# A fourth seven-product part and two overlapping GDN chains in a hybrid decoder layer on one Trainium2 core

## Chip, core and metric

The kernel runs on one core of a Trainium2 chip. The core has five engines with a queue of instructions each: PE (matrix products, with its weight loads shown as PEld), DVE (VectorE), ACT (ScalarE), POOL (GpSimd) and SP (SyncE, here only DMA issues). SP, ACT and POOL issue DMAs; 16 DMA engines carry them. The metric is the time of one execution on the device in microseconds (us), lower is better; 0.2% of it is 5.3 us.

## What is computed

One layer of a decoder trunk for 512 tokens and 2048 channels, in float32. Cut to what the change touches:

```python
h = _rmsnorm(x, norm_mix[l]) * (1.0 + sc_a) + sh_a
p = h @ w_in[l]                               # 2048 x 9296
c_q, c_kv, k_pe, q_g, k_g, v_g, z, b_logit, a_logit, gate_logits = _split_cols(p)
y_a = _mla_branch(c_q, c_kv, k_pe, ...) @ w_o_mla[l]
qkv = jnp.concatenate([q_g, k_g, v_g], axis=-1)          # 3 x 1024 columns, 8 heads of 128
y_b = _gdn_branch(qkv, z, b_logit, a_logit, ...) @ w_o_gdn[l]
...
def _gdn_branch(qkv, z, b_logit, a_logit, conv_w, ...):
    qkv = _causal_conv_silu(qkv, conv_w)      # width 4, along the tokens, per channel
    q, k = _l2norm(...), _l2norm(...)
    o = _gated_delta_chunked(q, k, v, beta, g)
    ...                                       # norm, times silu(z)

def _gated_delta_chunked(q, k, v, beta, g):
    ...
    Lmat = jnp.where(strict, jnp.einsum('bhncd,bhnsd->bhncs', kb, k) * decay, 0.0)
    sol = lax.linalg.triangular_solve(Lmat + I, rhs, lower=True, unit_diagonal=True)
    attn = jnp.where(lower, jnp.einsum('bhncd,bhnsd->bhncs', q, k) * decay, 0.0)
    def step(S, inp):                         # a scan over the chunks
        v_new = u_c - w_c @ S
        o = (q_c * exp(G_c)) @ S + a_c @ v_new
        S = S * exp(G_last) + k_dec.T @ v_new
```

After the two branches come the sigmoid gates, the output product, and a SwiGLU block that takes the second half of the time.

## The kernel before

**How it is written.** A Python program writes the whole instruction list. A matrix product is a list of *units* (`Unit`): a load of a weight tile, its split into a rounded part `hi` and a rest `lo` (ACT casts `hi`, DVE subtracts `lo`), and the matmuls, three for each pair of tiles (hi x hi, hi x lo, lo x hi). `Driver.run` writes the units in order, with loads and splits some units ahead (`drv.ahead`, `drv.deep`). Beside the units run *chains*, Python generators: after every 12 weighted matmuls (`GROUP`; a unit's `weight` is 1, `FAST` = 4/3, or 2) `pump` steps each chain once, and what the chain writes lands in the instruction order at that place. `yield n` in a chain is a pause of n pumps. `Score.order` then fixes the order on DVE and ACT with a model of times; PE, POOL and SP keep the written order.

**Interleaved loads.** `mixed` puts the units that read `w_mod` and some columns of `w_in` for the layer's modulation vectors (tiles `rawm`, `rawa`) between the others, at the pace of the table `PLAN`: pairs of (units before index n, such loads per unit). There are 160 of them.

**Buffers.** 68 tiles of 128 x 512 (`slots`), 5 weight tiles of 128 x 1024 (`raws`), 4 each for `hi` and `lo`, 8 PSUM banks. A tile's place is free again when its last reader is done, a store to DRAM included. The activations `hN` hold 32 of the 68 slots until gb3.

**Two ways to multiply.** A *plain set* (`w_in_fm`) makes 512 columns feature-major: 8 units of 24 matmuls, 192 in all, each 128 x 128 by 128 x 512. A *seven-product part* (`tokens_in`) makes 1024 columns token-major with seven block products in place of eight: 8 units of 4 products (24 matmuls) and 8 of 3 (18), 336 in all. A part's sums of weight blocks are made on DVE; one block sum goes out to `s_dram` from POOL and comes back. It uses sums and differences of the activations (`x56`, `x3`, parts of `hN`), which the part marked `last` gives up; `restore` then brings the overwritten halves of `hN` back.

**Order before** (`mixing`, line 2173 on): ga8, ga12; gb0 with the narrow set kb; three parts (latent queries and keys/values; Z; first halves of GDN queries and keys); then plain sets v03, q47, k47, v47, gb1, gb2, gb3; then the products of the attention (qpe, v0, v1, qk), ya, yb and the output product. In the names, 03 is heads 0 to 3 and 47 heads 4 to 7.

**GDN.** The token-major first halves of queries and keys stay in SBUF and are turned by 32 PE transposes (`inT`) at the start of v03. Convolved tiles (`conv_tile`, one per pump) of heads 0 to 3 stay in SBUF, those of heads 4 to 7 go to `cv_dram` and come back. `gdn(g)` is the chain of four heads: per chunk of 128 tokens it turns keys and queries (`pk`, `pq`), makes `kdec`, then turns values (`vp`), makes the decays `E`, the matrices `LT` and `AT`; then a solve of 31 steps on DVE (`fsX`, `fsT`), small products that build the inverse (`M1`, `X1`, `M2`, `X2`, `TT`), and a scan over the four chunks (`pks`, `r`, `pqs`, `py`, `yd`, `pS`, `po`, `o`). `kdec`, `vp`, `AT`, `kT` and `qT` stay in SBUF from start to end. The chain of heads 0 to 3 starts at v03, that of heads 4 to 7 in gb1, and `gated_out` follows each.

Of the kernel before, what the change touches and what calls it, by code (L numbers as in the profile page):

```python
# [16 lines left out]
P = 128  # L17
T = 512
NT = 4
# [265 lines left out]
class Score:  # L285
# [13 lines left out]
    def __init__(self, tc):  # L299
        self.tc = tc  # L300
        self.ops = []

    def engine(self, name):

        score, real = self, getattr(self.tc.nc, name)

        class Writer:
            def __getattr__(self, f):
                call = getattr(real, f)
                return lambda *args, **kwargs: score.ops.append(Op(name, f, call, args, kwargs))  # L310

        return Writer()
# [180 lines left out]
def block_kernel(ctx: ExitStack, tc: tile.TileContext, a: dict, out):  # L493
# [30 lines left out]
    def side(dst, src, **kw):  # L524
        nc.gpsimd.dma_start(dst, src, **kw)
# [354 lines left out]
    def conv_tile(idx, p):  # L880
        acc = S("cv")
        nc.scalar.activation(acc[:], p[:], AF.Copy, scale=cw[:, 72 + idx:73 + idx])
        for w in (2, 1, 0):
            sft = 3 - w
            nc.vector.scalar_tensor_tensor(acc[:, sft:], p[:, :T - sft], cw[:, 24 * w + idx:24 * w + idx + 1],
                                           acc[:, sft:], op0=ALU.mult, op1=ALU.add)
        nc.scalar.activation(acc[:], acc[:], AF.Silu)
        if idx % 8 < 4:
            conv_out[idx] = acc
        else:  # L890
            side(cv_dram[idx // 8, idx % 4], acc[:])
            conv_out[idx] = None

    cv_dram = dram.tile([3, 4, P, 512], F32, name="cv_dram")

    def conv_back(j):
        res = []
        for i in range(4):
# [22 lines left out]
    ba = C("ba", [P, NT, 16])  # L921
    kpe = C("kpe", [P, NT, 64])
    hspill = dram.tile([8, 2, P, 256], F32, name="hspill")

# [154 lines left out]
    fso = [dram.tile([4, NT, 4, 32, 32], F32, name=f"fso{g}") for g in range(2)]  # L1079

    def gdn(g):
        hd = slice(4 * g, 4 * g + 4)
        def conved(*parts):
            while not all(8 * j + 4 * g + i in conv_out for j in parts for i in range(4)):
                yield

        yield from conved(0, 1)
        while "eG" not in G:
            yield
        if g:  # L1090
            kT, qT = conv_back(1), conv_back(0)
            yield 5
        else:
            qT, kT = ([conv_out.pop(b + i) for i in range(4)] for b in (0, 8))
            yield 2

# [10 lines left out]

        kdec, vp, LT, AT = [], [], [], []
        for c in range(NT):
            pk, pq = tr4(kT, c, "pk"), tr4(qT, c, "pq")  # L1110
            kd = S("kdec")
            nc.vector.tensor_tensor(h4(kd[:]), h4(pk[:]), bc(G["eS"][:, c, hd], P), ALU.mult)
            kdec.append(kd)
            sumsq(pk[:], ssk[:, c, hd])
            sumsq(pq[:], ssq[:, c, hd])
            yield
# [14 lines left out]

        nxt = decays(0)
        yield from conved(2)
        vT = conv_back(2) if g else [conv_out.pop(16 + i) for i in range(4)]
        yield 3 if g else 1
        for c in range(NT):
            pv = tr4(vT, c, "pv")
            v = S("vp")
            nc.vector.tensor_tensor(h4(v[:]), h4(pv[:]), bc(nk_[:, c, hd], P), ALU.mult)
            vp.append(v)  # L1140
            eh, el = nxt
            if c < NT - 1:
                nxt = decays(c + 1)
            yield
            pe = PS("pE")
# [22 lines left out]
            nc.gpsimd.tensor_tensor(h4(at[:]), h4(at[:]), tri4, ALU.mult)  # L1168
            AT.append(at)
        del vT  # L1170
        fsL = []
# [10 lines left out]
        nc.gpsimd.memset(fsX_[64:128, 256:512:17], 1.0)  # L1182
        yield 2
        for j in range(31):
# [9 lines left out]
        del fsX_, fsX, fsT, fsL  # L1194
        T32 = S("T32")
# [53 lines left out]
        for hf in range(2):  # L1249
# [8 lines left out]
            M2.append(m2)  # L1258
        yield 6
        for hf in range(2):  # L1260
# [9 lines left out]
        del T64, T64T, T32, T32T, M1, M2, LT  # L1270
        yield
        Sst = S("Sst")
        for c in range(NT):
            if c:
                pks = PS("pks")
# [3 lines left out]
                for i in range(4):  # L1279
                    nc.vector.scalar_tensor_tensor(r[:, tok(i)], pks[:, tok(i)], G["eG"][:, c, 4 * g + i:4 * g + i + 1],  # L1280
                                                   vp[c][:, tok(i)], op0=ALU.mult, op1=ALU.subtract)
                pqs = PS("pqs")
# [6 lines left out]
            else:  # L1289
                r = vp[0]  # L1290
            py = PS("py")
# [7 lines left out]
            if c < NT - 1:  # L1299
                pS = PS("pS")  # L1300
                for i in range(4):
                    mm(pS[:, tok(i)], kdec[c][:, tok(i)], yd[:, tok(i)], start=True, stop=True)
                for i in range(4):
# [6 lines left out]
            for i in range(4):  # L1310
                mm(po[:, tok(i)], AT[c][:, tok(i)], yd[:, tok(i)], start=True, stop=True)
            o = S("o")
# [870 lines left out]
    def mixing():  # L2183
        yield act(load_scalars)
        for first, n in ((8, 4), (12, 4)):
# [7 lines left out]
            yield from us  # L2193
        us = w_in_fm("gb0", O_GB, gate_done(0), order=K_ORDER)
        for i, u in enumerate(us):
            def ahead(i=i):
                if i == 0:
                    for k in range(KT):
                        hT[k] = None
                while hN[K_ORDER[min(i + 2, 7)] + 1] is None:  # L2200
                    drv.step(chains["h"])
            with_pre([u], ahead)
# [12 lines left out]
        yield from tokens_in(0, O_CQ, c_out)  # L2215
        yield from tokens_in(1, O_Z, z_out)
        first = {}

        def first_out(t, f, src):
            dst = src  # L2220
            if src.tensor.name.startswith("m"):
                x = S("qk")
                dst = x[:]
                nc.scalar.copy(dst, src)
            first[t, f] = dst

        def turned_in():
            for f in range(2):
                for i0 in (0, 2):
                    both = [PS("inT") for _ in range(2)]  # L2230
                    for i, p in enumerate(both, i0):
                        for t in range(NT):
                            nc.tensor.transpose(p[:, tok(t)], first[t, f][:, tok(i)], ident)
                    conv_start(8 * f + i0, both)
                    yield
                for t in range(NT):
                    del first[t, f]
        yield from tokens_in(2, O_Q, first_out, O_K, lambda: drv.add(turned_in()), last=True)

        def start_conv():  # L2240
            drv.ahead = LOADS
            chains["conv"] = drv.add(conv_gen())
        us = with_pre(w_in_fm("v03", O_V, conv_done(16)), start_conv)
        with_pre(us[1:], gdn_sums)

        def start_a():
            ch["A"] = drv.add(gdn(0))
            drv.add(gated_out(0))
        with_pre(us, start_a)
        for u in us[4:]:  # L2250
            u.weight = FAST
        yield from us
# [4 lines left out]
        def start_b():  # L2257
            ch["B"] = drv.add(gdn(1))
            drv.add(gated_out(1))
        us = w_in_fm("gb1", O_GB + 512, gate_done(1), weight=FAST)  # L2260
        with_pre(us[2:], start_b)
        yield from us
        yield from w_in_fm("gb2", O_GB + 1024, gate_done(2), weight=FAST)
        us = w_in_fm("gb3", O_GB + 1536, gate_done(3), weight=FAST)
        for i, u in enumerate(us):
            def free(i=i):
                hN[2 * i] = hN[2 * i + 1] = None
            with_post(u, free)
            if i in (2, 4):
                with_pre([u], lambda i=i: chains.__setitem__(("q", "kv")[i // 2 - 1], drv.add(lora("q", n_qa) if i == 2 else lora("kv", n_kva))))  # L2270
        yield from us
# [1002 lines left out]
```

## Time and profile before

| | us |
|---|---|
| median of 3 runs | 2657.86 |
| lowest, highest | 2654.96, 2660.13 |
| profiled execution | 2656.74 |
| its span, first to last instruction | 2655.0 |
| granted TensorE clock in it | 0.999 |

From the starts of their first and last matmuls the stages of interest stand so in the profiled execution:

| stage | us |
|---|---|
| gb0 with kb | 188 to 243 |
| three seven-product parts | 243 to 473 |
| v03, q47, k47, v47 | 473 to 673 |
| gb1, gb2, gb3 | 673 to 841 |
| qpe, v0, v1 | 844 to 883 |
| qk, and ya | 883 to 1091 |
| scan of the first GDN chain (`py` to `po`) | 685 to 724 |
| scan of the second | 894 to 938 |

Lines of the profile name an engine, an operation, and what is written from what (out<-in). All of them carry line 483, where every recorded operation is issued, so tiles are told apart by name. A group has its count, busy time, mean length in ns, and the idle time before it with what ended it. A plain set's matmuls are `q`, `k`, `v` and `gb`, those of a part are `m`.

### The profile page before, as it was taken

The numbers are of one execution on the slowest core, as the hardware profiler recorded it, in microseconds if no ns is written. First come the engines' busy times: TensorE is split into PE (matmuls) and PEld (weight loads), VectorE is DVE, ScalarE is ACT, GpSimd is POOL, SyncE is SP. The second block draws the span as 40 slices with busy tenths as digits, with TensorE's granted clock in tenths as the row PEclk, the third lists the DMA queues.
The fourth block names the chain that finished last, engine by engine and source line by source line (L and its number), as shares of the span: only waits on it lengthen the run. The fifth ranks groups of instructions, "written<-read, shape, count | busy, mean of one in ns | idle before, by whom it ended". The sixth has DMA issues, their size and how long they took to land.

```text
span 2655.0 us, 36603 instructions
## 1 busy us (share of the span) xinstructions
PE 2635.5 (99%) x12668; PEld 2192.8 (83%) x12668; DVE 2215.8 (83%) x3401; ACT 1292.6 (49%) x1986; POOL 220.6 (8%) x369
## 2 busy tenths in 40 slices
PE   9999999999999999999999999999999999999998
PEld 7888888888888898888888888888888888888887
DVE  8988888878688688888997888888887888877888
ACT  4355444634535675234573444444444445445445
POOL 0000101011021000000100000000000101010000
PEclk9999999999999999999999999999999999999999
DMA  9985778755577447936854667766666667686795
GB/s 353 349 281 182 244 263 279 244 159 187 199 244 231 126 166 264 332 108 214 305 179 145 230 238 240 254 231 232 227 226 201 215 226 273 199 267 209 230 300 203
DMA packets 319986, 614.37 MB, mean 231 GB/s; under 512 B 45748, under 2 KB 74740, under 8 KB 319800
## 3 DMA queue, kind: packets, MB, share of 16 engines
q1 hardware_dynamic: 275064, 507.24, 58.0%
q0 software_dynamic: 24944, 78.97, 8.3%
q10 hardware_dynamic: 19792, 25.83, 2.9%
q8 instruction: 99, 1.62, 0.3%
q14 instruction: 87, 0.71, 0.1%
HBM read 518.55 MB, written 92.30 MB: 230 GB/s over the span
## 4 chain that ended last, share of the span: by engine, by line
PE 81%; issue 6%; DMA 5%; DVE 5%; ACT 2%; POOL 0%; ACTq 0%; SPq 0%; DVEq 0%; POOLq 0%
PE m L483 51%; PE v L483 4%; PE gu L483 3%; PE yb L483 3%; PE ya L483 3%; DMA raw<-in_w_in_dram 3%; PE gb L483 3%; PE q L483 2%; PE dn L483 2%; PE k L483 2%; PE dnt L483 2%; PE qk L483 2%; DVE lo L483 1%; DVE rawm L483 1%; ACT hi L483 1%
## 5 line engine op out<-in xcount | busy, mean ns | idle before, releaser
L483 ACT CAST hi<-raws 128x512 fp32r<-128x512 f32 (+1 forms) x448 | 409.1, 915 | 630.9 <-PE m L483 314.8
L483 DVE TENSOR_TENSOR lo<-raws,hi 128x512 fp32r<-128x512 f32 (+1 forms) x448 | 464.4, 1055 | 149.4 <-ACT hi L483 144.5
L483 ACT CAST hi<-raw 128x1024 fp32r<-128x1024 f32 (+2 forms) x199 | 201.9, 1017 | 306.4 <-DMA raw<-in_w_in_dram 75.1
L483 DVE TENSOR_TENSOR lo<-raw,hi 128x1024 fp32r<-128x1024 f32 (+2 forms) x199 | 234.1, 1181 | 62.5 <-ACT hi L483 60.6
L483 PE MATMUL m<-hi,xh 128*128 128x512 f32 x672 | 261.7, 389 | 1.2 <-ACT euvw L483 1.1
L483 PE MATMUL m<-hi,xl 128*128 128x512 f32 x672 | 261.4, 389 | 0.0
L483 PE MATMUL m<-lo,xh 128*128 128x512 f32 x672 | 261.4, 389 | 0.0
L483 ACT CAST hi<-sums 128x1024 fp32r<-128x1024 f32 x152 | 159.7, 1052 | 134.7 <-PE m L483 119.1
L483 DVE TENSOR_TENSOR lo<-sums,hi 128x1024 fp32r<-128x1024 f32 x152 | 185.6, 1221 | 38.0 <-ACT hi L483 38.0
L483 DVE CUSTOM_DVE_ANT_0 rawm<-rawm,cbc 128x1024 f32<-128x1024 f32 x160 | 195.3, 1238 | 15.3 <-DMA rawm<-in_w_mod_dram 15.0
L483 DVE TENSOR_TENSOR sums<-raws,raws 128x1024 f32<-128x1024 f32 x152 | 185.6, 1221 | 20.9 <-DMA raws<-in_w_down_dram 9.1
L483 PE MATMUL m<-hi,h2h 128*128 128x512 f32 x480 | 188.7, 393 | 0.0
L483 POOL DMA_DIRECT2D s_dram<-raws x152 | 82.3, 541 | 1263.5 <-DVE raws L483 1239.5
L483 PE MATMUL m<-hi,h2l 128*128 128x512 f32 x480 | 187.0, 389 | 0.0
L483 PE MATMUL m<-lo,h2h 128*128 128x512 f32 x480 | 186.8, 389 | 0.0
L483 PEld LDWEIGHTS m<-hi,xh 128*128 128x128 f32 x672 | 126.2, 188 | 28.2 <-ACT euvw L483 2.0
L483 PEld LDWEIGHTS m<-hi,xl 128*128 128x128 f32 x672 | 126.1, 188 | 26.3
L483 PEld LDWEIGHTS m<-lo,xh 128*128 128x128 f32 x672 | 126.2, 188 | 26.0
L483 DVE TENSOR_TENSOR raws<-raws,raws 128x512 f32<-128x512 f32 x152 | 103.2, 694 | 26.8 <-DMA raws<-in_w_down_dram 9.6
L483 DVE TENSOR_TENSOR raws<-sums,raws 128x512 f32<-128x512 f32 x152 | 104.6, 688 | 1.9
L483 PEld LDWEIGHTS m<-hi,h2l 128*128 128x128 f32 x480 | 90.1, 188 | 18.9
L483 PEld LDWEIGHTS m<-lo,h2h 128*128 128x128 f32 x480 | 90.2, 188 | 18.1
(555 smaller groups left out, 6396.3 us busy)
## 6 DMA issues: line engine op xcount, KB each, us to landing
raws<-in_w_gate_up_dram SPq DMA_DIRECT2D x400, 256.0 KB, 4.0
rawm<-in_w_mod_dram SPq DMA_DIRECT2D x160, 512.0 KB, 5.6
raw<-in_w_in_dram SPq DMA_DIRECT2D x95, 512.0 KB, 5.2
raws<-in_w_down_dram SPq DMA_DIRECT2D x160, 256.0 KB, 5.0
s_dram<-raws POOLq DMA_DIRECT2D x152, 256.0 KB, 3.7
raws<-s_dram SPq DMA_DIRECT2D x152, 256.0 KB, 3.9
raws<-in_w_in_dram SPq DMA_DIRECT2D x120, 256.0 KB, 4.3
raws<-in_w_o_dram SPq DMA_DIRECT2D x80, 256.0 KB, 4.1
```

Source lines behind the costliest of these rows:

```text
L483: self.tc.keep_in_program_order(op.call(*op.args, **op.kwargs))
```

## The change

The second halves of queries and keys (q47, k47) become a fourth part. The parts' order is now: latents; first halves; second halves; Z (which is `last`). The results of the two q/k parts go to `p_dram`, and one chain (`turn_first`), which starts at the tenth unit of Z, reads them back and turns them with 64 transposes. v03 takes gb0's place beside kb, and gb0 comes after v47 with weight `FAST`. All 24 convolved tiles are stored; first-half queries and keys are used from SBUF first, and all chains read values, and later queries and keys again, from DRAM. Both GDN chains are added at v47. Each stores `kdec`, `vp` and `AT` (11 tiles; the last chunk's `kdec` is no longer made) and drops `kT` and `qT` after the front, and reads them back for the scan. The set `mid` orders them: the second begins when the first is in the third of four chunks, the second's inverse when the first's scan is in its third chunk. `pause` waits for so many ns of matmul time by the planner's count. `PLAN` gets new paces, and the two latent chains start at gb3's units 0 and 3 in place of 2 and 4.

```diff
@@ conv_tile
-        if idx % 8 < 4:
-            conv_out[idx] = acc
-        else:
-            side(cv_dram[idx // 8, idx % 4], acc[:])
-            conv_out[idx] = None
+        side(cv_dram[idx // 8, idx % 8], acc[:])
+        conv_out[idx] = acc if idx in (0, 1, 2, 3, 8, 9, 10, 11) else None
@@ gdn
+        def keep(j, c, t):
+            side(gdn_dram[g, j, c], t[:])
+        def back(c):
+            res = []
+            for j in (0, 1, 2) if c < NT - 1 else (0, 1):
+                x = S(("vp", "AT", "kdec")[j])
+                nc.scalar.dma_start(x[:], gdn_dram[g, j, c])
+                res.append(x)
+            return res
-        while "eG" not in G:
+        while "eG" not in G or (g and "loops" not in mid):
             yield
+        while g and 0 not in mid:
+            yield
+        vT = conv_back(2, g)
...
+            if c == NT - 2:
+                mid.add("loops")
...
-        del vT
+        del vT, kT, qT, v, at, kd, eh, el, nxt, E, lt
+        mid.add(g)
...
-        yield 2
+        yield from pause(10000.0)
         for j in range(31):
...
-            if j % 4 == 3:
+            if j % 8 == 7:
                 yield
+        yield from pause(34000.0)
...
-        yield 24 if g else 22
+        yield from pause(11000.0)
+        while g and "second" not in mid:
+            yield
...
-        yield 6
+        yield 1
+        while not (g or 1 in mid):
+            yield
+        kT, qT, cur = conv_back(1, g), conv_back(0, g), back(0)
+        yield 5
...
         for c in range(NT):
+            if c == 2 and not g:
+                mid.add("second")
+            vp, AT, kdec = cur if c < NT - 1 else cur + [None]
+            if c < NT - 1:
+                cur = back(c + 1)
@@ plan
-    PLAN = ((17, 2.0), (33, 0.0), (81, 0.4), (89, 2.0), (113, 0.5), (137, 1.2), (143, 1.0), (156, 0.0), (175, 1.8), (1000, 1.2))
+    PLAN = ((17, 2.0), (33, 0.0), (89, 0.4), (97, 0.0), (113, 0.5), (137, 1.5), (143, 1.0), (156, 0.0), (175, 2.0), (1000, 1.5))
@@ mixing
-        us = w_in_fm("gb0", O_GB, gate_done(0), order=K_ORDER)
+        us = w_in_fm("v03", O_V, conv_done(16), order=K_ORDER)
...
-        yield from tokens_in(1, O_Z, z_out)
-        yield from tokens_in(2, O_Q, first_out, O_K, lambda: drv.add(turned_in()), last=True)
+        def turned_in(n, f, base):
+            rows = []
+            for t in range(NT):
+                x = S("tk")
+                nc.scalar.dma_start(x[:], p_dram[n, f, t])
+                rows.append(x)
+            yield 5
+            for i0 in (0, 2):
+                both = [PS("inT") for _ in range(2)]
+                for i, p in enumerate(both, i0):
+                    for t in range(NT):
+                        nc.tensor.transpose(p[:, tok(t)], rows[t][:, tok(i)], ident)
+                conv_start(base + i0, both)
+                yield 3
+        def turn_first():
+            yield from turned_in(0, 0, 0)
+            yield from turned_in(0, 1, 8)
+            gdn_sums()
+            yield
+            yield from turned_in(1, 0, 4)
+            yield from turned_in(1, 1, 12)
+        yield from tokens_in(1, O_Q, part_out(0), O_K)
+        yield from tokens_in(2, O_Q + 512, part_out(1), O_K + 512)
+        us = tokens_in(3, O_Z, z_out, last=True)
+        with_pre(us[9:], lambda: drv.add(turn_first()))
+        yield from us
...
-        yield from w_in_fm("q47", O_Q + 512, conv_done(4), weight=FAST)
-        yield from w_in_fm("k47", O_K + 512, conv_done(12), weight=FAST)
-        yield from w_in_fm("v47", O_V + 512, conv_done(20), weight=FAST)
+        def start_gdn():
+            drv.ahead = LOADS
+            for g in range(2):
+                ch["AB"[g]] = drv.add(gdn(g))
+                drv.add(gated_out(g))
+        yield from with_pre(w_in_fm("v47", O_V + 512, conv_done(20), weight=FAST), start_gdn)
+        yield from w_in_fm("gb0", O_GB, gate_done(0), weight=FAST)
+        yield from w_in_fm("gb1", O_GB + 512, gate_done(1), weight=FAST)
```

More of the change, by code (lines that the diff above doesn't have):

```diff
@@ L301, in __init__ @@
         self.ops = []
+        self.time = 0.0
     def engine(self, name):
@@ L309, in __getattr__, with record @@
                 call = getattr(real, f)
-                return lambda *args, **kwargs: score.ops.append(Op(name, f, call, args, kwargs))
+                def record(*args, **kwargs):
+                    op = Op(name, f, call, args, kwargs)
+                    score.ops.append(op)
+                    score.time += op.pace if op.pe else 0.0
+                return record
         return Writer()
@@ L887, in conv_tile, with conv_back @@
         nc.scalar.activation(acc[:], acc[:], AF.Silu)
-        if idx % 8 < 4:
-            conv_out[idx] = acc
-        else:
-            side(cv_dram[idx // 8, idx % 4], acc[:])
-            conv_out[idx] = None
-    cv_dram = dram.tile([3, 4, P, 512], F32, name="cv_dram")
-    def conv_back(j):
+        side(cv_dram[idx // 8, idx % 8], acc[:])
+        conv_out[idx] = acc if idx in (0, 1, 2, 3, 8, 9, 10, 11) else None
+    cv_dram = dram.tile([3, 8, P, 512], F32, name="cv_dram")
+    def conv_back(j, g):
         res = []
-        for i in range(4):
+        for i in range(4 * g, 4 * g + 4):
             x = S("cv")
@@ L1079, in block_kernel, with pause @@
     fso = [dram.tile([4, NT, 4, 32, 32], F32, name=f"fso{g}") for g in range(2)]
+    def pause(ns):
+        until_ = score.time + ns
+        while score.time < until_:
+            yield
+    gdn_dram = dram.tile([2, 3, NT, P, 512], F32, name="gdn_dram")
+    mid = set()
     def gdn(g):
         hd = slice(4 * g, 4 * g + 4)
+        def keep(j, c, t):
[7 more added lines that the diff above has]
+            return res
         def conved(*parts):
@@ L1132, in gdn @@
         nxt = decays(0)
-        yield from conved(2)
-        vT = conv_back(2) if g else [conv_out.pop(16 + i) for i in range(4)]
-        yield 3 if g else 1
+        yield 4
         for c in range(NT):
@@ L1194, in gdn @@
         del fsX_, fsX, fsT, fsL
+        yield from pause(7000.0)
         T32 = S("T32")
@@ L1301, in gdn @@
                 for i in range(4):
-                    mm(pS[:, tok(i)], kdec[c][:, tok(i)], yd[:, tok(i)], start=True, stop=True)
+                    mm(pS[:, tok(i)], kdec[:, tok(i)], yd[:, tok(i)], start=True, stop=True)
                 for i in range(4):
@@ L2215, in mixing @@
         yield from tokens_in(0, O_CQ, c_out)
-        yield from tokens_in(1, O_Z, z_out)
[L2217 to L2237, printed above, removed]
@@ L2253, in mixing, with part_out, output @@
-        yield from w_in_fm("q47", O_Q + 512, conv_done(4), weight=FAST)
-        yield from w_in_fm("k47", O_K + 512, conv_done(12), weight=FAST)
-        yield from w_in_fm("v47", O_V + 512, conv_done(20), weight=FAST)
[L2257 to L2262, printed above, removed]
+        def part_out(n):
+            def output(t, f, src):
+                dst = src
+                if src.tensor.name.startswith("m"):
+                    x = S("qk")
+                    dst = x[:]
+                    nc.scalar.copy(dst, src)
+                side(p_dram[n, f, t], dst)
+            return output
```

47 lines of the change are left out of this document (20 added, 27 removed).

## The prediction

> **What bounds the kernel now.** I read the page's busy table first, then the shares of the chain that ended last, then that chain in order of time.
>
> ```profile
> span 2655.0 us, 36603 instructions
> PE 2635.5 (99%) x12668; PEld 2192.8 (83%) x12668; DVE 2215.8 (83%) x3401; ACT 1292.6 (49%) x1986; POOL 220.6 (8%) x369
> PE 81%; issue 6%; DMA 5%; DVE 5%; ACT 2%; POOL 0%; ACTq 0%; SPq 0%; DVEq 0%; POOLq 0%
> ```
>
> PE is busy all along and carries 81% of the chain. That alone does not say that fewer matmuls are less time, since a modelled end can hide a wait. The chain in order of time does (start, length, what, how many):
>
> ```profile
> 476.28 0.87 PE inT L483 x8
> 479.90 0.87 PE inT L483 x8
> 484.18 0.87 PE inT L483 x8
> 487.80 0.87 PE inT L483 x8
> 580.54 43.52 PE k L483 x192
> 1178.89 76.22 PE m L483 x336
> 1493.47 68.02 PE m L483 x300
> ```
>
> 300 matmuls take 68.02 us, 192 take 43.52, 336 take 76.22: 226.7 ns each in every one, over 40 us and more on end. PE streams at a fixed pace there. The first four rows are all 32 transposes that turn the first halves of queries and keys: 8 in 0.87 us, 109 ns each. The view of what PE waited for, from 300 to 1010 us, says how much is not streaming:
>
> ```profile
> PE gb L483 <- DVE lo L483: 1.2, 2, 0.8
> PE py L483 <- DVE r L483: 1.1, 1, 1.1
> PE pT L483 <- ACT P L483: 1.0, 2, 0.7
> PE m L483 <- ACT up L483: 0.8, 1, 0.8
> PE sc L483 <- ACT P L483: 0.4, 1, 0.4
> PE m L483 <- DVE lo L483: 0.3, 1, 0.3
> ```
>
> In all 4.8 us out of 710 (columns: total, times, longest). So what is to be won is PE instructions, and waits can give back only a few us. What the other engines have left, by stretches (PE, PEld, DVE, ACT, POOL busy; clock; DMA share; GB/s):
>
> ```profile
> 0.00:100.00 100.00, 96.34 (x410) 77.56 (x411) 84.94 (x163) 45.20 (x60) 3.80 (x11) 1.00 0.96 350
> 243.00:319.00 76.00, 76.00 (x339) 62.98 (x338) 62.88 (x91) 38.20 (x48) 6.46 (x12) 1.00 0.66 225
> 319.00:396.00 77.00, 75.93 (x334) 62.06 (x333) 64.90 (x78) 34.56 (x43) 7.21 (x14) 1.00 0.78 267
> 396.00:473.00 77.00, 77.00 (x342) 63.75 (x341) 66.90 (x79) 34.62 (x43) 12.54 (x16) 1.00 0.83 283
> 440.00:473.00 33.00, 33.00 (x148) 27.31 (x147) 29.51 (x38) 15.72 (x21) 3.23 (x2) 1.00 0.91 307
> 473.00:842.00 369.00, 367.82 (x2069) 310.23 (x2068) 298.73 (x586) 177.17 (x400) 53.53 (x67) 1.00 0.65 207
> ```
>
> 243 to 473 are the three seven-product parts of now, 473 to 842 the seven plain sets from v03 to gb3 with the first GDN chain and the front of the second. The granted clock is 1.00 in each, so no count below needs a clock.
>
> **The change, part by part.**
>
> *Products.* The sets q47 and k47 go: 2 x 192 matmuls, 2 x 43.52 = 87.04 us. A fourth part comes: 8 units of 4 products and 8 of 3, each x 2 token tiles x 3 matmuls, 336 in all, 76.22 us. Its token-major results have to be turned, 32 transposes more, 4 x 0.87 = 3.48 us. Sum on PE: -87.04 + 76.22 + 3.48 = **-7.34 us**. That gb0 and v03 change places, Z comes last of the parts and the GDN matmuls move changes no PE count.
>
> *Waits of a part.* The `up` and the `lo` wait of `m` above, 1.1 us, are those of three parts: +0.4 for a fourth.
>
> *VectorE.* What a part costs it, from the page's groups, with the group that goes, from the groups of 476 to 930 us:
>
> ```profile
> L483 DVE TENSOR_TENSOR lo<-raws,hi 128x512 fp32r<-128x512 f32 (+1 forms) x448 | 464.4, 1055 | 149.4 <-ACT hi L483 144.5
> L483 DVE TENSOR_TENSOR lo<-sums,hi 128x1024 fp32r<-128x1024 f32 x152 | 185.6, 1221 | 38.0 <-ACT hi L483 38.0
> L483 DVE TENSOR_TENSOR sums<-raws,raws 128x1024 f32<-128x1024 f32 x152 | 185.6, 1221 | 20.9 <-DMA raws<-in_w_down_dram 9.1
> L483 DVE TENSOR_TENSOR raws<-raws,raws 128x512 f32<-128x512 f32 x152 | 103.2, 694 | 26.8 <-DMA raws<-in_w_down_dram 9.6
> L483 DVE TENSOR_TENSOR raws<-sums,raws 128x512 f32<-128x512 f32 x152 | 104.6, 688 | 1.9
> L483 DVE TENSOR_TENSOR lo<-raw,hi 128x1024 fp32r<-128x1024 f32 x67 | 81.5, 1222 | 24.0 <-ACT hi L483 23.5
> L483 DVE CUSTOM_DVE_ANT_0 rawm<-rawm,cbc 128x1024 f32<-128x1024 f32 x27 | 34.7, 1292 | 4.7 <-DMA rawm<-in_w_mod_dram 4.7
> ```
>
> A part has 8 each of the middle four and 24 of the first: 8 x (1.221 + 1.221 + 0.694 + 0.688) + 24 x 1.055 = 55.9 us, and 8 corrections of PSUM results, which I put at 0.69 like the nearest row (an estimate), 5.5: 61.4. Gone are 16 splits of q47 and k47, 16 x 1.222 = 19.6, and two `kdec` products, 1.4. So +40 us beside PE work. From 243 to 842 us VectorE is busy 62.88 + 64.90 + 66.90 + 298.73 = 493 of 599 us. The new pace table holds about 10 of the interleaved loads of `w_mod` back to after the queries' and keys' stage (34 + 0.4 x 56 + 0.5 x 16 + 1.5 x 24 + 6 = 106 by then, against 116): 10 x 1.29 = -13. Both chains now end about where gb3 ends, which brings the second chain's tail in, some 20 us on both VectorE and PE. Then (493 + 40 - 13 + 20) / (599 - 7 + 20) = 540 of 612, 88% where it was 82%. From 440 to 473 us it runs at 29.51 of 33, 89%, and PE is at 33.00 of 33: I cost it at nothing, and what hides it is the matmul stream. Without that cover it costs up to the whole 40.
>
> *DMA.* A part moves 48 loads and 8 stores of 0.262 MB, 14.7 MB, where two sets load 8.4: +6.3. Stores from POOL: 16 of the two parts' rows, 12 more convolved tiles, 22 GDN tiles; loads on ACT's queue: 16 rows, 20 more convolved tiles, 22 GDN tiles. That is 108 x 0.262 = 28.3 MB. Ten loads less of 0.524 are -5.2. From 243 to 842 us the rows give 76 x 0.225 + 77 x 0.267 + 77 x 0.283 + 369 x 0.207 = 136 MB; with +29 it is 165 in 612 us, 270 GB/s. Parts run without a wait at 283 and 307, the first 100 us reach 350. On average it is covered. The pinch is the end of the fourth part, below.
>
> *Issue and order.* The view of the tile `cv_dram`, the nearest to all these copies:
>
> ```profile
> L483 POOL DMA_DIRECT2D cv_dram<-cv x12: 539/542/583, 587.9 to 682.5; - x12
> L483 ACTq DMA_DIRECT2D cv<-cv_dram x12: 326/404/1750, 681.6 to 721.2; - x12
>   ACT yd L483: 3.7, 1
> DMA to landing us min/median/max: 2.3/3.3/7.4
> ```
>
> POOL gets 50 x 0.542 = 27 us more, ACT's queue 58 x 0.404 = 23; SP 32 more issues for the part. POOL is busy 53.5 of 369 us and ACT 177, so both have room. The added wait is that of an ACT load for the store of its tile to land. Behind it on ACT stand the casts `hi` of the next weights, and PE waits for these one or two units (5 to 10 us) later. Stores are issued tens of us before their load, except for the last four convolved tiles: between 0 and the 3.7 us that ACT `yd` once waited, on ACT alone; on PE I take 0.
> A store from POOL has a rule against it: the Trainium skill, "SBUF — State Buffer", Who interferes with whom, says that POOL cannot write a DMA's descriptors while a VectorE operation in a two-port mode holds the shared port, and gives 620 ns grown to 3100 beside a copy. By it 50 stores would land up to 2.5 us later each, an estimate from that page, and the time would be the slower rival's below instead of the sum's. The trace has no such gap in the issue (539 to 583 ns), only the spread of the landings, 2.3 to 7.4.
>
> *The chains.* The second starts when the first has two chunks of its front left, instead of after it. Its scan then no longer lies under the `qk` units, where `py` waited 1.1 us for `r` and `pT` 1.0 for `P`: -2.1. Against that, the solve of the second chain cost PE the 1.2 us of `gb` on `lo`; with two chains among the plain sets I take it twice: +1.2. Bounds: 0 to 12 us of new waits (one of 1.1 in eleven of 16 chunk rounds), and nothing below the 4.8 us of waits that there are.
>
> **Sum.** -7.34 + 0.4 - 2.1 + 1.2 = -7.8. The profiled execution took 2656.74 us (span 2655.0 and 1.7 around it): 2648.9. The median of the runs shown is 1.1 higher, 2657.86, and the forecast for a median is **2650.0**. From 2647 to 2653 it is the same case.
>
> **Rivals.**
>
> *More.* The waits of `gb`, `py` and `pT` (3.3 us) all go and none come: -7.3 + 0.4 - 3.3 = -10.2, 2647.6, or 2645 if ACT's `P` and `up` go too. For it: the scans leave the attention. Against: the solve's DVE operations are the same 31 steps.
>
> *The same: the DMA engines are full at the end of the fourth part.* In its last 33 us fall 4.7 MB of its own weights, 1.0 of v47's, 1.7 of interleaved loads, 0.5 of z, 2.1 of restored activations, 2.1 of rows to turn and 1.6 of convolved tiles: 13.7 MB, 417 GB/s. At the 350 of the first 100 us it is 2.2 MB or 6.3 us too much. The parts load two units ahead, 2 x 18 x 0.2267 = 8.2 us, which hides it; if that cover is gone, PE stands for 6.3: -7.8 + 6.3 = -1.5, **2656.4**. For it: the end of the last part is at 307 GB/s and share 0.91 already. Against: v47 takes no interleaved load now, which leaves its stretch at about 260.
>
> *Slower: slots.* All GDN tiles, rows and convolved tiles live in one pool of 68 tiles, and a tile is free only when its store has landed. The one place where that reached PE, in the chain:
>
> ```profile
> 898.94 5.77 DMA o_dram<-o
> 904.73 0.36 DVE r L483
> 905.22 1.17 PE py L483 x8
> ```
>
> `r` had to wait for a slot until `o` had landed, and PE lost the 1.1 us of the row above. Two chains with 22 kept tiles each going out and back make 16 chunk rounds. If each loses 1.1: 17.6, so -7.3 + 0.4 + 17.6 = +10.7, **2668.5**. From 7 rounds the gain is gone, from 12 it is slower by more than 0.2%. Against: the kept tiles leave the pool at once, so fewer are held than when `kdec`, `vp` and `AT` of a chain stayed.
>
> That the part does not do what it says is no rival of weight: the counts are in the code, and a part took 76.22 us wherever it ran unhindered.
>
> **How the numbers follow.** Forecast 0.50, more 0.10, same 0.24, slower 0.16. About 0.2% (5.3 us) is what a measurement of this kernel can tell from no change, so faster means under 2652.5: nearly all of the forecast's range (0.47) and more (0.10), 0.57; same is the DMA rival and the forecast's upper end, 0.27; slower 0.16. The range goes from 2644, below *more*, to 2662, where half of the slower case is in.
>
> **What would show it.** Right: 336 more `m`, 384 fewer `q` and `k`, 32 more `inT`, 226.7 ns still in the chain's long pieces, all parts in some 306 us; waits of PE from 300 to 1010 us again near 5 us; no `py` on `r` under `qk`. Wrong: `m` or `v` waiting on `hi` and a DMA at the end of the fourth part (the same), waits of `pkk`, `py`, `pS` for tiles whose slot waits on a store (slower), or VectorE over 95% in the stretch of both chains with `lo` as the releaser.

## The result, and the profile after

| | us |
|---|---|
| after, median of 4 runs (lowest, highest) | 2676.82 (2675.41, 2678.60) |
| before, median of 4 runs beside them | 2658.05 |
| ratio after / before | 1.0074, 95% interval 1.0061 to 1.0086 |
| profiled execution of after, its span | 2676.04, 2674.3 |

The change costs some 19 us where 8 were to be won. From the page of after, the span, the busy table and the DMA totals (rows of after carry line 490 where those of before carry 483):

```profile
span 2674.3 us, 36928 instructions
PE 2642.3 (99%) x12652; PEld 2196.4 (82%) x12652; DVE 2252.0 (84%) x3447; ACT 1298.1 (49%) x2004; POOL 250.0 (9%) x427
DMA packets 335540, 649.00 MB, mean 243 GB/s; under 512 B 48116, under 2 KB 77108, under 8 KB 335352
```

PE has 12652 instructions: 12668 - 384 + 336 + 32, as counted. So there is less to stream, and the time must have come from waiting. The windows say in which stage (PE, PEld, DVE, ACT, POOL busy; clock; DMA share; GB/s). First before, then after:

```profile
243.00:550.00 307.00, 305.93 (x1397) 253.56 (x1396) 266.04 (x363) 155.46 (x250) 30.15 (x44) 1.00 0.74 250
550.00:880.00 330.00, 328.82 (x2065) 277.03 (x2064) 261.16 (x535) 153.91 (x326) 50.75 (x68) 1.00 0.65 204
880.00:1000.00 120.00, 117.91 (x747) 105.15 (x746) 88.54 (x243) 89.78 (x211) 3.35 (x7) 1.00 0.44 139
1178.60:1333.80 155.20, 153.91 (x683) 127.00 (x681) 141.01 (x195) 84.91 (x123) 15.58 (x29) 1.00 0.72 242
```

```profile
243.00:550.00 307.00, 307.00 (x1372) 254.46 (x1372) 265.03 (x336) 148.93 (x189) 32.36 (x60) 1.00 0.79 269
550.00:880.00 330.00, 316.30 (x2057) 266.71 (x2056) 272.77 (x564) 163.94 (x415) 76.40 (x107) 0.96 0.78 257
1193.10:1353.20 160.10, 156.48 (x683) 128.42 (x681) 143.61 (x199) 84.28 (x123) 15.65 (x29) 0.98 0.72 235
```

The four parts (243 to 551) run without a gap. The stretch behind them, with v47, gb0 to gb3 and both GDN chains, loses 13.7 of its 330 us in PE's busy time and has a clock of 0.96; the output product (the last row of each) takes 4.9 us longer. Who ended PE's waits between 550 and 900 us, in after (total, times, longest):

```profile
PE pk L490 <- DMA cv<-cv_dram: 4.8, 2, 3.3
PE cT L490 <- ACT ckv L490: 2.3, 1, 2.3
PE M L490 <- issue: 1.7, 1, 1.7
PE M L490 <- ACT sg L490: 1.2, 1, 1.2
PE M L490 <- ACT T L490: 1.0, 1, 1.0
...
PE py L490 <- ACT eq L490: 0.5, 1, 0.5
```

The first five are 11.0 us, where the same view of before has only 1.2 (`gb` on `lo`). One of these places closely, windows of 5 us of after, and then ACT's timeline there (start, length, what, [idle before]):

```profile
640.00:645.00 5.00, 5.00 (x23) 4.14 (x23) 0.50 (x4) 0.00 (x0) 0.00 (x0) 1.00 1.03 395
645.00:650.00 5.00, 3.01 (x14) 2.10 (x12) 1.31 (x2) 1.04 (x1) 0.00 (x0) 1.00 1.05 376
650.00:655.00 5.00, 2.23 (x8) 2.04 (x9) 3.70 (x5) 1.85 (x8) 0.00 (x0) 0.51 0.97 263
```

```profile
636.85 10.72 ACTq L490 DMA_DIRECT2D cv<-cv_dram  x6
647.61 1.04 ACT L490 CAST hi<-raw 128x1024 fp32r<-128x1024 f32 x1 [10.13 <-DMA cv<-cv_dram]
```

The DMA engines are full (share 1.03) and ACT and DVE stand still, DVE at 0.50 of 5 us: ACT issues six loads of convolved tiles in 10.72 us, and behind them stands the cast `hi` of the next weights. In the trace such a load goes out right behind the landing of an earlier transfer: one at 638.55 after a store that landed at 638.48, the next at 641.42 after one at 641.40, both POOL's stores of the last convolved tiles. The longest stop is the sixth load's: it goes out at 647.24, behind a load of `rawa` that SP had issued at 637.93 and that landed at 647.17; in this trace SP's and ACT's transfers take turns on eight completion semaphores, and the sixth load takes the one of that `rawa`. Then PE's turn (its timeline):

```profile
649.15 0.33 PE L490 MATMUL pk<-kc,cv 128*128 128x128 f32 x1 [1.47 <-DMA cv<-cv_dram]
652.77 0.47 PE L490 MATMUL pk<-kc,cv 128*128 128x128 f32 x1 [3.29 <-DMA cv<-cv_dram]
...
654.75 0.63 PE L490 MATMUL gb<-hh,hi 128*128 128x512 f32 x1
655.17 0.63 PE L490 MATMUL gb<-hl,hi 128*128 128x512 f32 x1
655.60 0.63 PE L490 MATMUL gb<-hh,lo 128*128 128x512 f32 x1
656.03 0.63 PE L490 MATMUL gb<-hh,hi 128*128 128x512 f32 x1
```

Behind the gap matmuls start 427 ns apart instead of 227, with the granted clock at 0.51: a gap is paid a second time in slow matmuls.

To add this up I take for every two neighbouring matmuls the distance of their starts beyond the median distance of their kind (same shape and same tile written), and call the sum the **loss**. Its parts by stretch of each profiled execution, and the number of the 66 windows of 5 us from 550 to 880 with a DMA share of 0.95 or more (**full**):

| kernel | 240-540 | 540-900 | 900-1180 | 1180-1360 | rest | full |
|---|---|---|---|---|---|---|
| before | 1.8 | 5.9 | 4.1 | 2.1 | 2.9 | 13 |
| after | -0.2 | 31.4 | 1.2 | 7.0 | 2.7 | 25 |

Before to after, the loss grows by 25.4; less the 7.3 of products, 18.1, against 19.3 in the spans. Of what came after 240 us (13.4 before, 39.2 after), gaps of over 0.7 us are 5.2 and 16.7, and matmuls of 512 columns at half pace none and 37, 7.4 us.

### The profile page after: what moved, and what is told of

Read it like the earlier page. It is cut to its first block, busy times and chain, and to the rows that moved or that the text cites. A ratio compares the mean times of both kernels' runs of the same rounds, so it can differ in the third digit from the quotient of the medians.

```text
span 2674.3 us, 36928 instructions
## 1 busy us (share of the span) xinstructions
PE 2642.3 (99%) x12652; PEld 2196.4 (82%) x12652; DVE 2252.0 (84%) x3447; ACT 1298.1 (49%) x2004; POOL 250.0 (9%) x427
## 4 chain that ended last, share of the span: by engine, by line
PE 85%; DMA 6%; issue 4%; DVE 3%; ACT 1%; ACTq 0%; SPq 0%; POOL 0%; DVEq 0%; POOLq 0%
PE m L490 52%; PE v L490 4%; PE gu L490 3%; PE ya L490 3%; PE ga L490 3%; PE yb L490 3%; PE s L490 3%; PE gb L490 2%; PE dn L490 2%; PE qk L490 2%; PE dnt L490 2%; DMA rawa<-in_w_in_dram 1%; PE sc L490 1%; DMA raws<-in_w_down_dram 1%; DMA raw<-in_w_in_dram 1%
## 5 line engine op out<-in xcount | busy, mean ns | idle before, releaser
L490 ACT CAST hi<-raws 128x512 fp32r<-128x512 f32 (+1 forms) x472 | 430.5, 915 | 666.1 <-PE m L490 338.1
L490 DVE TENSOR_TENSOR lo<-raws,hi 128x512 fp32r<-128x512 f32 (+1 forms) x472 | 487.9, 1051 | 153.8 <-ACT hi L490 148.2
L490 ACT CAST hi<-raw 128x1024 fp32r<-128x1024 f32 (+2 forms) x183 | 185.0, 1014 | 257.9 <-DMA raw<-in_w_in_dram 93.7
L490 PE MATMUL m<-hi,xh 128*128 128x512 f32 x704 | 274.5, 390 | 1.6 <-ACT euvw L490 1.6
L490 PE MATMUL m<-lo,xh 128*128 128x512 f32 x704 | 274.4, 390 | 0.1
L490 PE MATMUL m<-hi,xl 128*128 128x512 f32 x704 | 274.4, 390 | 0.0
L490 DVE TENSOR_TENSOR lo<-raw,hi 128x1024 fp32r<-128x1024 f32 (+2 forms) x183 | 216.6, 1188 | 48.0 <-ACT hi L490 38.8
L490 DVE TENSOR_TENSOR lo<-sums,hi 128x1024 fp32r<-128x1024 f32 x160 | 195.3, 1221 | 36.5 <-ACT hi L490 36.0
L490 DVE TENSOR_TENSOR sums<-raws,raws 128x1024 f32<-128x1024 f32 x160 | 195.2, 1220 | 23.0 <-DMA raws<-in_w_down_dram 7.8
L490 DVE CUSTOM_DVE_ANT_0 rawm<-rawm,cbc 128x1024 f32<-128x1024 f32 x160 | 195.2, 1237 | 13.8 <-DMA rawm<-in_w_mod_dram 13.4
L490 PE MATMUL gb<-hl,hi 128*128 128x512 f32 x256 | 106.2, 415 | 0.0
L490 PEld LDWEIGHTS m<-hi,h2l 128*128 128x128 f32 x480 | 90.1, 188 | 18.9
```

The source lines that it names most:

```text
L490: self.tc.keep_in_program_order(op.call(*op.args, **op.kwargs))
```

## The experiments

Theory: the 108 added copies (28.3 MB) fill the DMA engines in the stretch of convolution and GDN, and the chains and splits there come late. Rivals: the overlap of the two chains; ACT's queue standing on loads; the fourth part. The loss is that of the profiled execution, which can lie up to 3 us from the median. All ratios are against the kernel before on the same chip, at 2657.7 to 2657.9.

**Fewer interleaved loads in that stretch** (after, loads put off):

```diff
-    PLAN = (... (113, 0.5), (137, 1.5), (143, 1.0), (156, 0.0), (175, 2.0), (1000, 1.5))
+    PLAN = (... (113, 0.5), (137, 0.6), (143, 1.0), (156, 0.6), (175, 2.4), (1000, 1.5))
```

> The changed kernel with fewer interleaved loads while both GDN chains run: the pace in gb1 to gb3 is 0.6 a unit instead of 1.5, and the loads held back come later (0.6 under qk and the first of ya, 2.4 in the rest of ya). Nothing else differs. Bandwidth theory (the 16 DMA engines are full, so every load lands late): 22 loads of 0.52 MB less in 150 us is 11.5 MB of some 45, the three bursts of PE waits near 650, 820 and 845 us (18 us of the 25 lost) shrink to a few us, time 2660 +- 4. Queue theory (ACT's loads wait for an earlier DMA of SP to land, and ACT's casts wait behind them): fewer SP loads in flight too, waits halved, 2666 +- 4. Overlap theory (two chains at once are too much for the order on DVE and ACT, whatever the DMAs do): 2674 to 2678.

2681.96, ratio 1.0091 (1.0074 to 1.0108). `ya` begins at 984.3 instead of 996.6 in after: with less traffic the stretch is 12 us shorter, and its loss falls from 31.4 to 18.9. The loads come too late instead, and the time is above all three forecasts; PE's waits from 1170 to 1205 us:

```profile
PE m L490 <- ACT rowT L490: 6.9, 1, 6.9
```

Loss 1180-1360: 22.6. Less traffic does shorten the stretch, but the loads have no better place there.

**The reverse** (after, loads earlier):

```diff
-    PLAN = (... (89, 0.4), (97, 0.0), (113, 0.5), (137, 1.5), (143, 1.0), (156, 0.0), (175, 2.0), (1000, 1.5))
+    PLAN = (... (89, 0.65), (97, 0.3), (113, 0.5), (137, 0.7), (143, 1.0), (156, 0.0), (175, 2.2), (1000, 1.5))
```

> The changed kernel with interleaved loads taken out of gb1 to gb3 (0.7 a unit instead of 1.5) and put where the four parts run (0.65 instead of 0.4, and 0.3 in Z's second half), 2.2 instead of 2.0 in ya; e1_pace held them back too late, and lost at the output product what it won. Bandwidth theory: the win of e1_pace up to ya (12 us) without its loss, 2664 +- 4, if the parts bear 0.25 loads a unit more (they run at 0.85 of the DMA engines now). If the parts do not bear it: PE waits of m on lo or hi from 243 to 551 us, 2675.

2690.40, 1.0116 (1.0101 to 1.0132). Now the parts lose 17.7 (after: none), the stretch still 28.1. The parts had no room left either, and the time is above both forecasts.

**No overlap** (after):

```diff
-        while "eG" not in G or (g and "loops" not in mid):
+        while "eG" not in G or (g and ch["A"] in drv.chains):
...
-        while not (g or 1 in mid):
-            yield
```

> The changed kernel with the overlap of the GDN chains undone: the second chain starts when the first has ended, and the first no longer waits for the second's front. The fourth part and the tiles in DRAM stay. Overlap theory: the three bursts go, 2652 +- 4, less 1 to 4 us lost where the second chain's tail now lies under qk and ya. Bandwidth and queue theories: the same copies spread over some 150 us more, at about two thirds of the load: waits of PE from 600 to 900 us about a third of now, 2662 +- 5.

2676.35, 1.0072 (1.0057 to 1.0087): as after, where both forecasts were lower. The loss of 540-900 halves (15.5), and comes back elsewhere: 8.3 in 900-1180 (after: 1.2), 8.4 in the output product (7.0), 8.2 in the rest (2.7); the sum is 42.1 in both. Overlap decides where it is lost, not how much. That the same copies spread over a longer time cost as much is not explained by the theory alone.

**Traffic without the change** (the kernel before; the copies are of `w_mod` into a tensor that nobody reads, and wait for nothing, so the written order puts some from 432 us on):

```diff
+        def ballast():
+            for n in range(108):
+                side(bal_dram[n], w_mod[n % 6, tok(n // 6 % 16), 512 * (n % 4):512 * (n % 4) + 512])
+                yield
+        drv.add(ballast())
         yield from w_in_fm("q47", O_Q + 512, conv_done(4), weight=FAST)
```

> The kernel before, with the traffic alone: a chain beside the others copies 108 blocks of 0.262 MB from one DRAM tensor to another on POOL's queue, one per pump, from the start of q47 on (28.3 MB, as many as the change's stores and loads; the copies are never used). PE, DVE and ACT do what they did. Bandwidth theory: PE waits in 530 to 850 us grow from 5 to 15 us or more, 2670 +- 5. Queue theory (only loads that stand in ACT's queue hurt): 2659 +- 3. Overlap theory: 2658 +- 2.

2690.56, 1.0122 (1.0107 to 1.0137): +32.7 with none of the change in it, more than the theory's 2670. Its windows, the stage and then one burst:

```profile
550.00:880.00 330.00, 312.12 (x1807) 261.72 (x1807) 239.79 (x493) 135.03 (x290) 99.11 (x159) 0.97 0.83 268
```

```profile
790.00:800.00 10.00, 10.00 (x50) 8.38 (x49) 3.93 (x7) 2.00 (x2) 6.60 (x13) 1.00 1.00 299
800.00:810.00 10.00, 10.00 (x46) 8.28 (x45) 2.82 (x4) 1.53 (x2) 0.00 (x0) 1.00 1.01 351
810.00:820.00 10.00, 10.00 (x46) 8.29 (x45) 8.75 (x25) 6.66 (x10) 0.00 (x0) 1.00 1.00 328
820.00:830.00 10.00, 3.90 (x18) 2.89 (x16) 9.35 (x31) 2.06 (x6) 0.00 (x0) 0.85 0.16 60
```

Who waited there, ACT from 785 to 820 us, DVE from 788 to 812, PE from 815 to 840:

```profile
ACT hi L483 <- DMA raw<-in_w_in_dram: 20.6, 3, 10.8
```

```profile
DVE lo L483 <- ACT hi L483: 6.7, 2, 4.1
DVE rawm L483 <- DMA rawm<-in_w_mod_dram: 6.7, 3, 3.9
```

```profile
PE gb L483 <- DVE lo L483: 11.4, 1, 11.4
```

While the DMA engines are full, ACT waits 20.6 us for weights and DVE gets 3.93 and 2.82 of 10 us of work. Then the late splits and the solve (`fsX`, `fsT`) stand before DVE together, it works 9.35 of 10, and PE waits 11.4 us for a split at a moment when the DMA engines are at 0.16. DVE's timeline:

```profile
812.39 0.19 DVE L483 TENSOR_TENSOR fsT<-fsL,fsX 128x31 f32<-128x31 f32 x1 [0.47 <-DMA fsL<-fsd]
834.04 1.22 DVE L483 TENSOR_TENSOR lo<-raw,hi 128x1024 fp32r<-128x1024 f32 x1
```

The first row is the start of the solve, which had waited for the load of `fsL`; the second is the split that PE waits for. Its `hi` was ready at 810.4, but in DVE's order it stands behind nearly the whole solve, as it does in before, where the solve begins at 783.5. The releaser of that wait is DVE; its cause lies 20 us earlier, in the transfers.

Two limits. The planner, which knows of the copies, also chose another order for some instructions of DVE and ACT (the traces differ from before in 88 and 35 places, PE's order in none); with four copies, below, it is 27 and 18 places for 3 us. And 16 of the 108 copies went out from 432 to 465 us, at the end of the third part: the loss of 240-540 rises from 1.8 to 8.6, that of 540-900 from 5.9 to 27.7.

**Half the dose, and four copies** (the same, `range(54)` and `range(4)`):

> The kernel before with 54 instead of 108 copies of 0.262 MB from DRAM to DRAM, begun at q47. The 108 copies cost +32.7 us. Traffic in proportion: half of it, about +16 (2674), and the product of the output still a few us longer than 155. A knee (the engines become full only above some amount): under +8 (below 2666). A price of the start alone, whatever the amount: over +25 (above 2683).

> The kernel before with four such copies begun at q47: the same DRAM tile and the same remainder by eight in GpSimd's counters as with 108, hardly any traffic. If traffic makes the waits: 2657 to 2661, with wo to gu at 155 as before. If the loss of the output's product comes from the place of the tiles in DRAM or from the phase of the counters: wo to gu again at about 160 and the time near 2663.

54 copies: 2670.35, 1.0051 (1.0034 to 1.0068). Four: 2661.00, 1.0012 (1.0003 to 1.0021). So +3, +12.5 and +32.7 for 4, 54 and 108; the windows of four and of 54 copies (that of 108 is above):

```profile
550.00:880.00 330.00, 328.41 (x2063) 276.67 (x2062) 260.29 (x535) 153.01 (x325) 52.23 (x68) 1.00 0.66 204
```

```profile
550.00:880.00 330.00, 326.50 (x2017) 274.75 (x2016) 256.43 (x528) 145.60 (x311) 73.48 (x106) 0.99 0.75 234
```

At 0.66, 0.75 and 0.83 of the DMA engines, 11, 20 and 34 full windows and 6.2, 10.0 and 27.7 us of loss in 540-900. The time grows with the amount, the second half dearer than the first. The half dose, too, has 16 of its copies before 473 us, and loses 6.9 in 240-540. The output product takes 155.6 and 155.4 us with four and 54 copies: neither the new tensor in DRAM nor copies from POOL as such lengthen it.

**The same traffic elsewhere** (108 copies, begun at the first `qk` unit):

> The kernel before with the 108 copies begun at the first query-key product (883 us in the trace of before) instead of at q47. In that stage the DMA engines are 0.60 busy at 204 GB/s, in the stretch behind q47 0.65 at the same 204. If it is the amount that costs, wherever it falls: again about +33 (2690). If it is the place, the convolution's and GDN's waits on a full set of engines: under +15 (below 2673), and the bursts between 640 and 860 us are gone.

2667.53, 1.0036 (1.0025 to 1.0047). 94 of the 108 copies were issued between 880 and 1000 us:

```profile
880.00:1000.00 120.00, 116.24 (x729) 103.01 (x727) 81.03 (x223) 80.36 (x200) 53.33 (x102) 0.99 0.97 325
```

Engines 0.97 busy for 120 us cost less than a third of what the ballast at 0.83 over 330 us did: the loss of 900-1180 rises from 4.1 to 8.7, that of 540-900 from 5.9 to 8.6. Full engines alone are no price; what is due behind them is. In this stage DVE has 81 of 120 us of work, in the GDN's 261 of 330 and more, so a late load can be caught up here. That last reason is argued from these rows, not shown by a run of its own.

**Half the copies out of after** (one convolved tile read for four heads, the kept GDN tiles of the first chunk used for all; 56 copies fewer):

```diff
-        for i in range(4 * g, 4 * g + 4):
-            x = S("cv")
-            nc.scalar.dma_start(x[:], cv_dram[j, i])
-            res.append(x)
-        return res
+        x = S("cv")
+        nc.scalar.dma_start(x[:], cv_dram[j, 4 * g])
+        return [x] * 4
...
-            side(gdn_dram[g, j, c], t[:])
+            if c == 0:
+                side(gdn_dram[g, j, c], t[:])
...
```

> The changed kernel with half of the copies left out: each read-back of four convolved tiles loads one tile and uses it for all four heads, and of vp, AT and kdec only the first chunk's tile is stored and read back, and used for every chunk (so queries, keys, values and scan of most heads and chunks are not those of the layer). 24 + 16 loads and 16 stores fewer, 14.7 of 28.3 MB; PE, DVE and ACT compute as much as before, and fewer slots are held. Bandwidth theory: the bursts of PE waits near 650, 820 and 845 us shrink to under 6 us in all, 2660 +- 4. Overlap theory: 2674 +- 4. Part theory (the fourth part or its turning): 2674 +- 4.

2662.91, 1.0018 (1.0009 to 1.0028): 13.9 of the 18.8 us are back, with the part and the overlap of after in place. The run takes out more than bytes: ACT issues 40 loads fewer, and fewer slots are held. That bytes alone cost time is the ballast's part of the argument. The stage is at 237 GB/s, 19 full windows, and its loss at 18.2.

```profile
550.00:880.00 330.00, 322.64 (x2133) 274.73 (x2133) 283.38 (x584) 173.66 (x441) 69.84 (x91) 0.98 0.74 237
```

In this stretch that is some 8 us more than the half dose loses at the same fill (0.75, 20 full windows, loss 10.0). Over the whole execution the two are alike: +5.0 and 7.3 of products won make 12.3 here, the half dose costs 12.5, some 5 of it before 540 us. So these runs do not show that a copy costs more because a chain reads it back.

**The read-backs from another queue** (after; all loads from `cv_dram`, `gdn_dram` and `p_dram` issued by SP, then by POOL):

```diff
-            nc.scalar.dma_start(x[:], cv_dram[j, i])
+            nc.sync.dma_start(x[:], cv_dram[j, i])
...
```

> The changed kernel with all read-backs of convolved tiles, of GDN tiles and of the rows to turn issued by SP instead of ACT. The bytes, the tiles and the places in the written order are the same. Queue theory: ACT no longer stands still at a load, its casts and copies are on time, PE's waits on pk, M and cT mostly go: 2662 +- 5. Bandwidth theory: the same bytes at the same time, 2675 +- 4. Overlap theory: 2675 +- 4. A result over 2680 would say that SP's weight loads now wait behind the read-backs.

> The changed kernel with the same read-backs issued by POOL instead of ACT (e5_sp moved them to SP and gained 2 us). POOL's DMAs wait for other completion counters than those of SP and ACT, so neither the casts nor the weight loads stand behind them. Queue theory: 2665 +- 5. Bandwidth theory: 2676 +- 4.

SP: 2674.76, 1.0066 (1.0050 to 1.0081); POOL: 2688.13, 1.0116 (1.0099 to 1.0133). PE's waits from 550 to 900 us, SP, then POOL:

```profile
PE pk L490 <- ACT sq L490: 7.9, 1, 7.9
PE gb L490 <- DVE lo L490: 3.8, 2, 2.3
PE adac L490 <- DVE acc L490: 2.5, 1, 2.5
```

```profile
PE cT L490 <- ACT ckv L490: 7.6, 1, 7.6
PE pk L490 <- ACT sq L490: 2.8, 1, 2.8
```

Relieving ACT's queue takes the wait of `pk` for `cv` away and puts one of 7.9 us in its place; the interval of SP's ratio contains after's 1.0074, and POOL's time is above both forecasts. So ACT's queue is where the lack showed; that it is the cause is not borne out. SP's run has 36 full windows in the stretch where after has 25, and the same loss (30.7, after 31.4): the number of full windows is a sign and no price.

**Without the fourth part** (after, with q47 and k47 as plain sets again, between Z and v47):

```diff
-        yield from tokens_in(2, O_Q + 512, part_out(1), O_K + 512)
-        us = tokens_in(3, O_Z, z_out, last=True)
+        us = tokens_in(2, O_Z, z_out, last=True)
...
+        yield from with_pre(w_in_fm("q47", O_Q + 512, conv_done(4), weight=FAST), loads)
+        yield from w_in_fm("k47", O_K + 512, conv_done(12), weight=FAST)
```

> The changed kernel with the fourth part undone: q47 and k47 are plain sets again, between the last part (Z) and v47; the overlap and the tiles in DRAM stay. 7.3 us more PE work. If the part itself costs nothing but its PE time (all three theories above), 2684 +- 4: the PE waits of after stay where they are. If the part's own traffic, or the 64 transposes and the stores and loads of its rows, bring the waits, 2662 +- 5.

2682.78, 1.0096 (1.0081 to 1.0111), 6.0 more than after; the part is worth about its 7.3 us of PE time, and the loss of 540-900 stays (26.2). The harm is in the rest of the change.

No kernel here is faster than the one before. The version that the runs point to, the fourth part with the GDN's tiles left in SBUF, was not tried; whether its tiles would fit into the 68 slots is not shown.

## Why the prediction was wrong

It said 2650, from 2644 to 2662; it was 2676.8. The step that failed is **DMA**, with its sentence "On average it is covered".

- *Products*, -7.34: right. The counts are those of the page, and undoing the part cost 6.0.
- *Waits of a part*, +0.4: right in effect; the four parts lost nothing (-0.2, before 1.8).
- *VectorE*: 540 of 612 us was forecast, 88%; the rows give 265.03 + 272.77 of 637, 84%. The mean has room, as it said. But it named the matmul stream as cover for DVE's work, and not what feeds DVE: at 640 us it has 0.50 of 5 us to do, and what it did not do then comes too late.
- *DMA*: 270 GB/s was forecast; 269 and 257 were measured. The size was right and the conclusion wrong, since the mean was compared with the peak of other stages (283, 307, 350). The 28 MB alone, in the kernel before, cost 32.7 us at a mean of 268 GB/s. The windows in which the engines are full say more than the mean, 13 before and 25 after, though the loss does not follow their number from run to run.
- *Issue and order*: ACT was to wait up to 3.7 us, behind the stores of the last four convolved tiles, and PE not at all. The place was right; ACT stood 10.1 us on six loads, PE 4.8 and another 2 in slow matmuls. Over 5 us of ACT's stop were for an interleaved load, which the prediction did not name. The rule of the Trainium skill that was weighed there ("SBUF — State Buffer", Who interferes with whom) is not borne out: the added stores were issued at the old pace (count, then ns min/median/max):

```profile
L490 POOL DMA_DIRECT2D gdn_dram<-AT x8: 565/565/596, 597.8 to 715.2; - x8
L490 POOL DMA_DIRECT2D gdn_dram<-kdec x6: 542/542/542, 566.0 to 667.0; - x6
```

- *The chains*, -2.1: right; the loss of 900-1180 falls from 4.1 to 1.2, and `py` and `pT` wait no more under `qk`. Their +1.2 for new waits, with bounds of 0 to 12, measured 25.5 (5.9 to 31.4), 12.3 even with the copies halved (18.2). The bound counted rounds of the scan, one wait each; the waits came at the chains' fronts and solves, and several drew slow matmuls behind them, where the prediction had counted with a clock of 1.00 throughout.
- Not in the sum: the output product's +4.9.
- *Rivals*: the one called *the same* had the mechanism, full engines, but at the end of the fourth part, which ran free, and it priced one pinch of 6.3 us, not a stretch of 300 us in which one follows another. That price fits the end of the third part in the ballast and the half dose, where 16 copies fell on it and the loss of 240-540 rose by 6.8 and 5.1. *Slower* had the sign and about half of the size, by another mechanism, slots; the scans' rounds cost PE the 0.5 us of `py` above, not 17.6, and in after no wait of PE or DVE from 550 to 900 us ends with the landing of a store. The second chain's overlap, which fed both, is not what costs.

The sum with what was measured: -7.3 - 2.0 (parts) - 2.9 (`qk`) + 25.5 + 4.9 - 0.2 = +18.0; the spans differ by 19.3, so 1.3 us are not accounted for.

**Open.** The output product is the same work in all kernels and takes 155.2 to 156.2 us in before and with 4, 54 or 108 late copies, but 157.8 to 161.4 in after and its variants (where the put-off loads do not fall into it) and 159.9 with the full ballast. Its DMA share is not higher (0.72 both). What is left over from the stretch before was not found.

## What to carry to other kernels

A mean GB/s below the peak does not cover added transfers. Look at windows of a few us in the stage that takes them, count those in which the DMA engines are full, and ask which engine is starved there and whether it has the slack to catch up: the same 28 MB cost 33 us where VectorE and the splits had little to spare (24 MB of it in that stretch, the rest at the end of the part before), and 10 us in the next stage. And price an expected wait on PE at more than its length, because matmuls behind it can run at half pace.

## What the runs showed of the hardware

The granted clock falls after gaps shorter than I had thought. In after's output product (PE's timeline):

```profile
1312.73 0.39 PE L490 MATMUL m<-hi,xl 128*128 128x512 f32 x1
1314.92 0.50 PE L490 MATMUL m<-hi,a2h 128*128 128x512 f32 x1 [1.81 <-ACT euvw L490]
...
1318.77 0.80 PE L490 MATMUL m<-hi,xh 128*128 128x512 f32 x1 [1.59 <-ACT euvw L490]
1319.37 0.63 PE L490 MATMUL m<-lo,xh 128*128 128x512 f32 x1
1319.79 0.63 PE L490 MATMUL m<-hi,xl 128*128 128x512 f32 x1
1320.22 0.63 PE L490 MATMUL m<-hi,xh 128*128 128x512 f32 x1
1320.65 0.63 PE L490 MATMUL m<-lo,xh 128*128 128x512 f32 x1
```

1.81 and 1.59 us without work, and matmuls then start 427 ns apart; the granted clock is 0.50 from 1315.73 to 1322.56, so it fell before the second gap. The Trainium skill, "TensorE: Matmul & The Clock Gate", Part 1, gives an idle window of about 3.4 us for this; the measurement decides. Not every such gap does it: in before, whose longest after 240 us was 1.1 us, no matmul of 512 columns ran at that pace, and with the late copies gaps of 1.96 and 2.15 us, ending at 804 and 1311 us, left the clock at 1.00. In after it stayed at 0.50 for 3.4 to 10.2 us each time.

The DMA engines moved up to 407 GB/s in windows of 5 us of after (570 to 575 us, share 1.04) and 396 in before (690 to 695, share 1.05), above the 349 and 350 of the first 100 us.
